# Hybrid decoder block on one core: reordering the state-space octets among the projections

## Chip, core and metric

The kernel runs on one core of one Trainium2 chip. The metric is the device time of one execution in microseconds. Three executions of the kernel before took 2342.69, 2344.36 and 2347.79 us; their median, 2344.36 us, is the time before. Engines are named as in the profile: PE does matrix products (PEld its weight loads), DVE and ACT work on vectors, POOL is GpSimd, SP only issues transfers. SP, ACT and POOL can each issue DMAs, from queues of their own.

## What is computed

One decoder block on a sequence of 512 tokens with 2048 channels: an adaptive norm and one input projection, a diagonal state-space group (S5) and a sparse-attention group side by side, an output projection, and a gated feed-forward part. The change touches the S5 group, the order in which the projections and two "compressions" are put beside it, and some stores of keys and values. The reference of these, cut:

```python
def s5_mixer(u, ...):                      # 64 groups of 16 channels, 64 complex states each
    dt = exp(log_dt); mag = exp(lr * dt)
    ab = mag * cos(li * dt), mag * sin(li * dt)
    den = lr * lr + li * li
    f_re = ((ab_re - 1) * lr + ab_im * li) / den      # the factors of B
    f_im = (ab_im * lr - (ab_re - 1) * li) / den
    bb = f * b                                        # per group 64 x 16
    bu = einsum('bsgh,gph->sbgp', u, bb)
    states = associative_scan(a_l * a_r, a_r * b_l + b_r)   # over the 512 tokens
    y = real(states @ c) + d_skip * u
    z = gelu(y); return z * sigmoid(z @ w_glu + b_glu)

def compress_tokens(kv, pe, w1, w2):       # once for K, once for V
    flat = overlapping blocks of 32 tokens of kv + pe
    return gelu(flat @ w1) @ w2
```

## The kernel before

Weights and activations are f32; every large product is made as three products of halves (hi·hi, lo·hi, hi·lo: L100, L101, L102), so each weight tile `wr` is cast to `wh` on ACT and subtracted to `wl` on DVE (both L75), in two halves of 128x1024 for a projection. The kernel goes through phase A (to about 223 us), phase B1 (to about 499 us), the attention, the output projection, and the feed-forward part. The change lies at the end of phase A and in B1.

**Phase A.** While PE makes the products for `u`, K and V, POOL works from the start on the S5 tables (`s5_prep`, L59): powers of the discretised A, then a normalisation of two pairs of tables on 128x512 tiles (`n1`), the copies into `s5CH` and `s5SH`, and at the very end the three multiplications that finish the factors of B, `s5fr` and `s5fi`, by the reciprocal of `den`. At the end of phase A, four tiles of K (`qk_d`, 512 KB each, from `spill`, L675) and four of V (`v_d`, 256 KB each, L319) are stored to DRAM; these eight stores stand on POOL, behind the tables. They are read from the tiles `adw`, whose memory B1's S5 tiles take over.

**Phase B1.** Twelve projections `proj(i)` of 48 matmuls 128x512 each. Among them eight S5 octets (`s5_octet`, eight groups each). An octet, in the order of the code: `s5bb` and `s5bg`, `s5TT` from the factors of B and the tables (L526 to L549); the octet's C and S tables (`s5C`, `s5S`, `s5x`; L563 to L569); eight transposes (L585) that give `s5W`; `Kt` (16 transposes, L593), which is stored to `k_s` (L599) and read back in a skewed form as the weight `s5w` (L603; named `w3` in the code, one buffer); the bias `bu` from the weight tile `s5wt` and the row `shb` (L610 to L618); the input product E (L625); the scan with a product by a rotated identity (L638); the state `s5SS`; and the output Y (L647 with `s5w`, L648 with `s5SS`), gelu and the store `z_d` (L652). Octets are put after projections 2, 3, 5, 6, 8, 9, 11 by the rule `12 * n < 8 * (i - 1)`, and the last after the loop. `compress(0)` stands ahead of projection 11; then, behind the last octet, `gate` (31 matmuls, L744, L745), `compress(1)` (its transposes are L784, its weights `wh<-in_w_dram`), `gate_tail`.

**What sets the order.** Each engine takes its instructions strictly in one order. A scheduler makes it at build time from dependences and priorities (`high_priority`), with order-only links where the code asks for them (`after`, and `Held`, which links each operation of an engine to one before it). So an instruction that waits holds everything behind it on its engine, also what belongs to other work.

Of the kernel before, what the change touches and what calls it, by code (L numbers as in the profile page):

```python
# [64 lines left out]
class Block:  # L65
    def __init__(self, ctx, tc, a):
        self.ctx, self.tc, self.a = ctx, tc, a
        self.nc = tc.nc
        self.V, self.A, self.T = tc.nc.vector, tc.nc.scalar, tc.nc.tensor


# [8 lines left out]
    def weights(self, src, out=None, first=None):  # L80

        res = []
        with self.tc.high_priority():
            raw = self.wp.tile([P, 2048], F32, name="wr", bufs=2)
            self.nc.sync.dma_start(raw, src)
            for h in range(2):
# [6 lines left out]
                if first is not None:  # L93
                    self.after(parts, first)
                res.append((hi, lo))
        return res
# [114 lines left out]
    def phase_a(self, hh, hl, tab, ps):  # L211
# [4 lines left out]
        with ExitStack() as st:  # L216
# [59 lines left out]
            for kt in range(KT):  # L276
# [4 lines left out]
                if kt >= 8:  # L281
                    hl[kt] = tab.tile([P, S], F32R, name=f"hl{kt}")
                self.modulate(xt[kt], m[:, 1, kt:kt + 1], m[:, 0, kt:kt + 1], rb, hh[kt], hl[kt], pa)
                if kt < 8:
# [22 lines left out]
            for i in range(4):  # L307
                p = pk[i]
                if i == 0:
                    q, t = (pa.tile([P, 8, 64], F32, name="modt", bufs=2).rearrange("p a b -> p (a b)")  # L310
                            for _ in range(2))
                    p = self.rope(p, q, t, self.rot[:, 0], self.rot[:, 1], 64)
                if i % 2 == 0:
                    o = tmp(4).bitcast(F32R)
                self.spill(self.qk_d[0, P * i:P * i + P], p, o[:, 2 * (i % 2):2 * (i % 2) + 2])
            o = tmp(4)
            for t in range(4):
                A.copy(o[:, t], pk[4 + t])
                self.v_spill = nc.gpsimd.dma_start(self.v_d[t], o[:, t])  # L319

# [18 lines left out]
    def s5_prep(self, pool, W):  # L339
# [93 lines left out]
        with tc.high_priority(-100000):  # L433
# [6 lines left out]
            V.tensor_add(den, den, q)  # L440
            self.V.reciprocal(rd, den)
            V.tensor_scalar(nr, ar, -1.0, None, op0=ALU.add)
# [4 lines left out]
            V.tensor_add(fr, fr, q)  # L447
            V.tensor_mul(fr, fr, rd)
            V.tensor_mul(fi, ai, lr)
            V.tensor_mul(q, nr, li)  # L450
            V.tensor_sub(fi, fi, q)
            V.tensor_mul(fi, fi, rd)
            V.tensor_scalar(fi, fi, sgn, None, op0=ALU.mult)
            r8 = pool.tile([P, 64], F32, name="s5r8")
# [28 lines left out]
            powers(CA, SA, fc, fs)  # L483
            n1 = t((P, 8, 64))
            for C, Sn in ((CB, SB), (CA, SA)):

# [21 lines left out]
    def s5_octet(self, o, Tb, W, ps):  # L508
# [5 lines left out]
        U, bc = self.s5_next  # L514
        SS = W.tile([P, 8, 66], F32, name="s5SS")
        V.memset(SS[:, :, 0:1], 0.0)
        bx, cx = bc[:, 0], bc[:, 1]
# [41 lines left out]


        Ch, Sh = C[:, :, 0:4], Sn[:, :, 0:4]
        tc1 = W.tile([P, 8, 8, 8], F32, name="s5x", bufs=4)[:, :, 0:4]
# [5 lines left out]
        V.tensor_mul(tc2, ab(Tb["CH"]), ba(Tb["SB"]))  # L568
        V.tensor_add(Sh, Sh, tc2)  # L569
        for x, sg in ((C, 1.0), (Sn, -1.0)):  # L570
            A.activation(x[0:64, :, 4:8], x[64:P, :, 0:4], AF.Copy, scale=sg)
# [9 lines left out]
        with hp():  # L581
            for q in range(2):
                p = ps.tile([P, 4, P], F32, name="tp", bufs=2)
                for g in range(4):
                    T.transpose(p[:, g], w1[:, 4 * q + g].rearrange("p r i -> p (r i)"), self.ident)  # L585
                A.copy(W1[:, 4 * q:4 * q + 4], p)
        Kt = W.tile([P, 8, 9 * 16], F32, name="s5bg", bufs=3).rearrange("p a b -> p (a b)")
        Kt = Kt[:16, 0:1024].rearrange("p (g x) -> p g x", g=8)
# [53 lines left out]
        V.tensor_mul(z5, z3, Sf)  # L642
        V.tensor_add(SS[:, :, 1:65], z4.rearrange("p (g j) -> p g j", g=8), z5.rearrange("p (g j) -> p g j", g=8))
        with hp():
            Y = ps.tile([P, S], F32, name="acc", bufs=4)
            for g in range(8):
                T.matmul(Y[:, 64 * g:64 * g + 64], w3[:, g], U[:, g], start=True, stop=False)  # L647
                T.matmul(Y[:, 64 * g:64 * g + 64], TT[:, g, 0:8].rearrange("p k h -> p (k h)"), SS[:, g, 0:64],  # L648
                         start=False, stop=True)
            zz = W.tile([P, 8, 64], F32, name="s5x", bufs=4)  # L650
# [21 lines left out]

    def spill(self, dst, q, t, scale=None):
        self.split(q, t[:, 0], t[:, 1], scale)
        self.nc.gpsimd.dma_start(dst, t.bitcast(F32))  # L675

    def phase_b1(self, hh, hl):
        nc, tc, a, V, A, T = self.nc, self.tc, self.a, self.V, self.A, self.T
        with ExitStack() as st:
# [8 lines left out]
            shb = self.shb = W.tile([P, D], F32, name="shb")  # L688
            self.after([nc.gpsimd.dma_start(shb, self.sh_d.to_broadcast([P, D]))], self.v_spill)
            n = 0  # L690

            def octet(n):
                if n:
                    self.s5_next = self.s5_loads(n, SW)
                self.s5_octet(n, self.Tb, SW, ps)

            for i in range(12):
                if i == 11:
                    self.compress(0, W, ps)
                p = self.proj(i, hh, hl, ps)  # L700
                with tc.high_priority():
# [13 lines left out]
                    else:  # L715
# [5 lines left out]
                        self.spill(self.qk_d[g, P * t:P * t + P], p, t2, -0.125)  # L721
                while 12 * n < 8 * (i - 1):
                    octet(n)
                    n += 1
            octet(n)
            gs = self.gate(hh, hl, W, ps)
            self.compress(1, W, ps)
            self.gate_tail(gs, ps)
# [810 lines left out]
```

## Time and profile before

| | |
|---|---|
| median of three runs | 2344.36 us |
| the profiled execution, its own time | 2354.09 us |
| its span in the trace | 2352.3 us |
| PE busy | 2195.6 us, 93% |
| DVE busy | 1854.9 us, 79% |
| ACT busy | 1080.2 us, 46% |
| POOL busy | 309.6 us, 13% |

The profiled execution is one run; its time is 9.73 us above the median of the three others and 1.8 us above its own span. PE's share is that of the whole span: within phase B1 there are stretches with PE at nearly 100% and others with PE near 0, and the rows further below are taken stretch by stretch. "PEclk" in the rows is the granted TensorE clock as a share of full speed: 1.00 is 2.4 GHz, 0.50 is 1.2 GHz.

### The profile page before, as it was taken

How to read it: one execution, taken by the hardware profiler on the slowest of the kernel's cores; microseconds unless marked ns; L12 is line 12 of the kernel's file. 1: busy time of each engine (PE TensorE's matmuls, PEld its weight loads, DVE VectorE, ACT ScalarE, POOL GpSimd, SP SyncE). 2: the span in 40 equal slices, each digit the busy share in tenths (PEclk: the TensorE clock that was granted, in tenths of full speed). 3: DMA queues.
4: the chain of work that ended last, by engine and by line, in shares of the span. 5: the costliest groups of instructions: out<-in, count | busy, mean ns of one | idle time of the engine just before them, and what ended most of it. 6: DMA issues, size and time to landing. Idle time of an engine off the chain costs nothing.

```text
span 2352.3 us, 34734 instructions
## 1 busy us (share of the span) xinstructions
PE 2195.6 (93%) x13694; PEld 1918.0 (82%) x13694; DVE 1854.9 (79%) x2776; ACT 1080.2 (46%) x1823; POOL 309.6 (13%) x376
## 2 busy tenths in 40 slices
PE   7997899878899878899999999999999999999997
PEld 5776778666677666899999999999999788888886
DVE  7896888658988877889999999999999773553436
ACT  3422444348867742744445444454444431221215
POOL 8999111100000011000000000000000000000000
PEclk9999999979999989999999999999999999999998
DMA  9784656576477467233333333333333783443223
GB/s 345 289 284 177 207 167 177 158 209 207 150 239 228 171 258 287 85 123 127 126 129 126 122 122 122 122 121 122 122 121 112 286 310 120 148 145 119 90 90 108
DMA packets 94003, 398.20 MB, mean 169 GB/s; under 512 B 19968, under 2 KB 28448, under 8 KB 58384
## 3 DMA queue, kind: packets, MB, share of 16 engines
q1 hardware_dynamic: 79440, 344.51, 42.0%
q0 software_dynamic: 14400, 51.49, 6.6%
q8 instruction: 107, 1.75, 0.3%
q14 instruction: 56, 0.46, 0.1%
HBM read 358.20 MB, written 37.69 MB: 168 GB/s over the span
## 4 chain that ended last, share of the span: by engine, by line
PE 54%; issue 4%; DVE 3%; ACT 1%; DMA 1%; POOL 1%; POOLq 0%; DVEq 0%; ACTq 0%
PE dn L102 7%; PE dn L100 7%; PE dn L101 6%; PE sa L101 6%; PE sa L100 6%; PE sa L102 6%; PE sb L100 5%; PE sb L102 5%; PE sb L101 5%; DMA adw<-in_wada_dram 0%; DVE wl L75 0%; DMA a_d<-cv 0%; POOL adw L119 0%; POOL x_d L1045 0%; DVE cv L1090 0%
## 5 line engine op out<-in xcount | busy, mean ns | idle before, releaser
L75 ACT CAST wh<-wr 128x1024 fp32r<-128x1024 f32 (+1 forms) x257 | 262.0, 1024 | 502.5 <-PE dn L101 320.5
L75 DVE TENSOR_TENSOR wl<-wr,wh 128x1024 fp32r<-128x1024 f32 (+1 forms) x255 | 307.6, 1210 | 50.1 <-ACT wh L75 38.8
L124 DVE SCALAR_TENSOR_TENSOR adw<-adw,silc 128x2048 f32<-128x2048 f32 x63 | 146.7, 2331 | 26.4 <-DMA adw<-in_wada_dram 25.3
L100 PE MATMUL mm<-yh,wh 128*128 128x512 f32 (+1 forms) x320 | 129.4, 409 | 26.7 <-DVE x L1043 7.8
L75 ACT CAST xh<-wq 128x1024 fp32r<-128x1024 f32 x84 | 88.3, 1052 | 139.2 <-DVE wq L1229 104.2
L75 ACT CAST wh<-wq 128x1024 fp32r<-128x1024 f32 x84 | 88.3, 1052 | 137.8 <-DVE wq L1229 104.5
L1099 POOL DMA_DIRECT2D a_d<-cv x44 | 23.8, 541 | 856.5 <-DVE cv L1098 856.5
L101 PE MATMUL mm<-yl,wh 128*128 128x512 f32 (+1 forms) x320 | 128.8, 403 | 7.4 <-DVE yl L75 7.4
L102 PE MATMUL mm<-yh,wl 128*128 128x512 f32 (+1 forms) x320 | 127.9, 401 | 1.9 <-DVE wl L75 1.9
L1293 DVE SCALAR_TENSOR_TENSOR x<-dn,mod,x 128x512 f32<-128x512 f32 (+1 forms) x56 | 37.6, 673 | 108.3 <-PE dn L102 107.8
L75 DVE TENSOR_TENSOR xl<-wq,xh 128x1024 fp32r<-128x1024 f32 x84 | 102.4, 1218 | 24.2 <-ACT xh L75 24.2
L75 DVE TENSOR_TENSOR wl<-wq,wh 128x1024 fp32r<-128x1024 f32 x84 | 102.2, 1218 | 22.7 <-ACT wh L75 22.7
L100 PE MATMUL dn<-b21h,wh 128*128 128x512 f32 x256 | 101.8, 398 | 3.1 <-ACT wh L75 3.1
L102 PE MATMUL dn<-b21h,wl 128*128 128x512 f32 x256 | 102.1, 399 | 0.5 <-DVE wl L75 0.5
L1229 DVE TENSOR_TENSOR wq<-wq,wr 128x1024 f32<-128x1024 f32 x84 | 102.0, 1215 | 0.1
L101 PE MATMUL dn<-b21l,wh 128*128 128x512 f32 x256 | 101.8, 398 | 0.0
L100 PE MATMUL dn<-t4h,wh 128*128 128x512 f32 (+1 forms) x256 | 97.8, 382 | 0.0
L102 PE MATMUL dn<-t4h,wl 128*128 128x512 f32 (+1 forms) x256 | 97.7, 382 | 0.0
L101 PE MATMUL dn<-t4l,wh 128*128 128x512 f32 (+1 forms) x256 | 97.6, 381 | 0.0
L100 PEld LDWEIGHTS mm<-yh,wh 128*128 128x128 f32 x320 | 62.7, 198 | 41.7 <-issue 16.9
L146 POOL TENSOR_TENSOR rms_r<-rms_v,mhalf 128x2 f32<-128x2 f32 (+1 forms) x8 | 10.8, 1346 | 637.5 <-DVE rms_v L144 637.4
L102 PE MATMUL mm<-hh,wl 128*128 128x512 f32 x192 | 79.5, 414 | 15.9 <-DVE wl L75 15.9
(535 smaller groups left out, 7852.8 us busy)
## 6 DMA issues: line engine op xcount, KB each, us to landing
adw<-in_wada_dram SPq DMA_DIRECT2D x49, 1024.0 KB, 6.7
wr<-in_wup_dram SPq DMA_DIRECT2D x46, 1024.0 KB, 4.9
wq<-in_wup_dram SPq DMA_DIRECT2D x42, 1024.0 KB, 6.8
wr<-in_wdn_dram SPq DMA_DIRECT2D x40, 1024.0 KB, 4.9
wr<-in_wada_dram SPq DMA_DIRECT2D x32, 1024.0 KB, 4.9
wr<-in_wout_dram SPq DMA_DIRECT2D x16, 1024.0 KB, 5.5
adw<-in_wada_dram POOLq DMA_DIRECT2D x14, 1024.0 KB, 7.7
wr<-in_wp_dram SPq DMA_DIRECT2D x12, 1024.0 KB, 5.2
```

What stands on the lines that cost most here:

```text
L75: return self.A.copy(hi, src), self.V.tensor_sub(lo, src, hi.bitcast(F32))
L100: self.T.matmul(ps, wh, xh, start=start, stop=False)
L101: self.T.matmul(ps, wh, xl, start=False, stop=False)
L102: self.T.matmul(ps, wl, xh, start=False, stop=stop)
L124: self.V.scalar_tensor_tensor(t, t, 1.0, self.silc, op0=ALU.mult, op1=ALU.mult, accum_out=out)
L146: self.rms_pow = self.nc.gpsimd.tensor_tensor(r[:, 0:n], v[:, 0:n], self.mhalf.to_broadcast([P, n]), op=ALU.pow)
L1099: self.nc.gpsimd.dma_start(self.a_d[:, m], val)
L1229: V.tensor_add(src, src, add)
L1293: V.scalar_tensor_tensor(x, p, gate, x, op0=ALU.mult, op1=ALU.add)
```

## The change

- `s5_prep` gets a third step. The reciprocal of `den` is put on DVE behind the modulation of K-tile 8 of phase A, and the three multiplications of `s5fr` and `s5fi` stand on POOL ahead of the last normalisation instead of behind the copies.
- The four `qk_d` and four `v_d` stores at the end of phase A are issued by ACT; the load of `shb` is issued by SP, behind the loads of weights and of `rt`.
- In the first octet the C and S tables are linked behind a `wl` of the weights (`self.lo[-2]`), so that the octet begins with `s5bb`.
- `s5_octet` becomes a generator with two stops. Its first part goes to the copies of `s5W`; the second from the state's memset over `Kt`, `s5w`, E and the scan to `s5SS`; the third is Y, gelu and `z_d`. The third part of an octet is written out between the first and the second part of the next. Y's matmuls lose their high priority. The state's memset moves into the second part.
- The octets follow the rule `12 * n < 9 * (i - 1)`: after projections 2, 3, 4, 6, 7, 8, 10, 11. `compress(0)` stands ahead of projection 9, `compress(1)` ahead of projection 11. Behind the loop come `gate`, the Y of the last octet, and `gate_tail`.

The number of matmuls is the same.

```diff
@@ s5_prep @@
-            self.V.reciprocal(rd, den)
...
-            V.tensor_mul(fr, fr, rd)
...
-            V.tensor_mul(fi, fi, rd)
-            V.tensor_scalar(fi, fi, sgn, None, op0=ALU.mult)
...
             n1 = t((P, 8, 64))
+        yield
+        with tc.high_priority(-100000):
+            with tc.high_priority(200000):
+                self.after([self.V.reciprocal(rd, den)], self.modulated)
+            V.tensor_mul(fr, fr, rd)
+            V.tensor_mul(fi, fi, rd)
+            last = V.tensor_scalar(fi, fi, sgn, None, op0=ALU.mult)
+            V = Held(V, lambda i: self.after([i], last))
             for C, Sn in ((CB, SB), (CA, SA)):
@@ phase_a @@
-                self.spill(self.qk_d[0, P * i:P * i + P], p, o[:, 2 * (i % 2):2 * (i % 2) + 2])
+                self.spill(self.qk_d[0, P * i:P * i + P], p, o[:, 2 * (i % 2):2 * (i % 2) + 2], queue=nc.scalar)
...
-                self.v_spill = nc.gpsimd.dma_start(self.v_d[t], o[:, t])
+                nc.scalar.dma_start(self.v_d[t], o[:, t])
@@ s5_octet @@
-        SS = W.tile([P, 8, 66], F32, name="s5SS")
-        V.memset(SS[:, :, 0:1], 0.0)
...
+        if o == 0:
+
+            lo = self.lo[-2]
+            V = Held(V, lambda i: self.after([i], lo))
         Ch, Sh = C[:, :, 0:4], Sn[:, :, 0:4]
...
                 A.copy(W1[:, 4 * q:4 * q + 4], p)
+        yield
+        SS = W.tile([P, 8, 66], F32, name="s5SS")
+        V.memset(SS[:, :, 0:1], 0.0)
...
+        yield
+        Y = ps.tile([P, S], F32, name="acc", bufs=4)
+        for g in range(8):
+            T.matmul(Y[:, 64 * g:64 * g + 64], w3[:, g], U[:, g], start=True, stop=False)
...
         with hp():
-            Y = ps.tile([P, S], F32, name="acc", bufs=4)
...
@@ phase_b1 @@
-            self.after([nc.gpsimd.dma_start(shb, self.sh_d.to_broadcast([P, D]))], self.v_spill)
+            nc.sync.dma_start(shb, self.sh_d.to_broadcast([P, D]))
             n = 0
+            prev = []
...
-                self.s5_octet(n, self.Tb, SW, ps)
+                cur = self.s5_octet(n, self.Tb, SW, ps)
+                next(cur)
+                if prev:
+                    next(prev.pop(), None)
+                next(cur)
+                prev.append(cur)
 
             for i in range(12):
-                if i == 11:
-                    self.compress(0, W, ps)
+                if i in (9, 11):
+                    self.compress((i - 9) // 2, W, ps)
...
-                while 12 * n < 8 * (i - 1):
+                while 12 * n < 9 * (i - 1):
                     octet(n)
                     n += 1
-            octet(n)
             gs = self.gate(hh, hl, W, ps)
-            self.compress(1, W, ps)
+            next(prev.pop(), None)
             self.gate_tail(gs, ps)
```

How this moves instructions on the engines, at three places. First DVE at the end of phase A, before the change: the first octet's memset and tables stand ahead of the projection's second `wl`.

```order
L75 TENSOR_TENSOR adw<-b,adw 128x512 x2
L516 MEMSET s5SS 128x8
L563 TENSOR_TENSOR s5C<-s5CH,s5CB 128x8x32
L564 TENSOR_TENSOR s5x<-s5SH,s5SB 128x8x32
L567 TENSOR_TENSOR s5S<-s5SH,s5CB 128x8x32
L565 TENSOR_TENSOR s5C<-s5C,s5x 128x8x32
L568 TENSOR_TENSOR s5x<-s5CH,s5SB 128x8x32
L75 TENSOR_TENSOR wl<-wr,wh 128x1024
```

The same place after the change (line numbers are those of the changed kernel; its L76 is L75 before, L600 the memset):

```order
L76 TENSOR_TENSOR adw<-b,adw 128x512 x2
L600 MEMSET s5SS 128x8
L532 TENSOR_TENSOR s5bb<-s5bc,s5fr 128x128
L533 TENSOR_TENSOR s5tb<-s5bc,s5fi 128x128
L532 TENSOR_TENSOR s5bb<-s5bc,s5fr 128x128
L533 TENSOR_TENSOR s5tb<-s5bc,s5fi 128x128
L534 TENSOR_TENSOR s5bb<-s5bb,s5tb 128x128
L536 TENSOR_TENSOR s5bb<-s5bb,s5tb 128x128
L538 TENSOR_SCALAR s5bc<-s5bc,cons 128x128
L537 TENSOR_SCALAR s5bb<-s5bb,cons 128x128
L548 TENSOR_TENSOR s5bg<-s5bb,s5PR 128x8x128
L549 TENSOR_TENSOR s5bg<-s5bb,s5PI 128x8x128
```

The next instruction behind these is the `wl` that stood behind the tables before. The memset, which waited for nothing before, now takes memory that the `v_d` stores read, and waits for these. On PE the first octet's eight transposes, which had 77 of the projections' matmuls ahead of them, have 42.

POOL at the end of the tables, before: the factors of B, the eight stores and `shb` stand behind the last copies.

```order
L59 COPY s5SH<-sp_1060 64x256 x2
L59 TENSOR_TENSOR s5fr<-s5fr,sp_1005 128x64
L59 TENSOR_TENSOR s5fi<-s5fi,sp_1005 128x64
L59 TENSOR_SCALAR s5fi<-s5fi,cons 128x64
L675 DMA qk_d<-adw 128x1024 x2
L319 DMA v_d<-adw 128x512
L675 DMA qk_d<-adw 128x1024 x2
L319 DMA v_d<-adw 128x512 x3
L689 DMA shb<-sh_d 128x2048
```

ACT at the end of phase A, after the change: the stores stand between the copies out of PSUM, ahead of the next weights' cast.

```order
L76 CAST adw<-b 128x512 x2
L322 COPY adw<-b 128x512
L690 DMA qk_d<-adw 128x1024 x3
L323 DMA v_d<-adw 128x512
L322 COPY adw<-b 128x512 x2
L323 DMA v_d<-adw 128x512 x2
L322 COPY adw<-b 128x512
L323 DMA v_d<-adw 128x512
L76 CAST wh<-wr 128x1024
```

The stores leave POOL's queue; ACT, on which a waiting issue holds the casts of the weights, takes them over.

PE near the end of B1, before: the Y of the octet before the last (L647) stands directly behind that octet's scan product (L638), in the middle of projection 11's matmuls.

```order
L100 MATMUL mm<-hh_118,wh 128x512
L585 MATMUL tp<-cons,s5bg 128x128 x4
L638 MATMUL acc<-s5x,cons 128x512
L647 MATMUL acc<-s5U,s5w_3630 128x64
L585 MATMUL tp<-cons,s5bg 128x128 x4
L101 MATMUL mm<-hl_1754,wh 128x512
L102 MATMUL mm<-hh_118,wl 128x512
```

PE at the end of B1, after the change: the last matmuls of the gate, the last octet's L652 (L638 before), and its Y.

```order
L764 MATMUL mm<-hl_1754,wh 64x512
L765 MATMUL mm<-hh_118,wh 128x512
L764 MATMUL mm<-hl_1794,wh 64x512
L765 MATMUL mm<-hh_120,wh 128x512
L652 MATMUL acc<-s5x,cons 128x512
L661 MATMUL acc<-s5U,s5w_3813 128x64
L662 MATMUL acc<-s5SS,s5TT 128x64
```

POOL in the same stretch, after the change: the last `s5w` is issued behind the store of the octet before it.

```order
L613 DMA k_s<-s5bg 128x1x128
L690 DMA qk_d<-sp 128x1024
L667 DMA z_d<-s5x 8x128x64
L617 DMA s5w_3813<-k_s 128x8x128
L667 DMA z_d<-s5x 8x128x64
```

The last `s5w` is read into the one buffer that the Y before it still reads, so it comes behind that Y. Before the change, `compress(1)` stood between the gate and the gate's tail; now the last Y stands there, and the Y of the octet before it stands ahead of the gate.

## Rows read from the trace of the kernel before

**Rows 1.** Waits of PE from 205 to 500 us: line, releaser, total us, times, longest.

```profile
PE mm L102 <- DVE wl L75: 15.9, 1, 15.9
PE acc L647 <- DMA s5w<-k_s: 7.9, 1, 7.9
PE tp L784 <- DMA wh<-in_w_dram: 6.3, 1, 6.3
PE acc L638 <- DVE bu L613: 2.7, 1, 2.7
```

**Rows 2.** Stretches: busy us (instructions) by engine, PEclk, DMA share, GB/s.

```profile
223.00:239.00 16.00, 0.07 (x2) 0.03 (x1) 3.79 (x7) 2.18 (x5) 12.56 (x21) 0.64 0.42 156
262.00:446.00 184.00, 176.97 (x965) 143.96 (x963) 156.00 (x265) 84.71 (x181) 23.93 (x27) 0.98 0.60 173
446.00:455.00 9.00, 1.11 (x5) 0.52 (x4) 3.80 (x4) 0.00 (x0) 1.33 (x1) 0.69 0.30 60
455.00:475.00 20.00, 19.66 (x106) 14.26 (x105) 8.56 (x19) 9.72 (x25) 3.73 (x4) 0.88 0.46 127
...
482.00:499.00 17.00, 14.74 (x85) 12.99 (x85) 6.50 (x22) 6.14 (x13) 1.27 (x1) 0.80 0.79 172
330.00:360.00 30.00, 27.62 (x142) 22.73 (x141) 22.24 (x38) 12.98 (x27) 4.32 (x5) 0.89 0.68 196
390.00:420.00 30.00, 29.70 (x160) 24.42 (x158) 27.56 (x46) 11.19 (x24) 4.34 (x5) 1.00 0.70 210
```

**Rows 3.** Timeline of DVE: start, us, line, operation, idle before and releaser.

```profile
216.77 0.07 DVE L516 MEMSET s5SS<- 128x8 f32 x1
...
235.82 0.61 DVE L564 TENSOR_TENSOR s5x<-s5SH,s5SB 128x256 f32<-128x256 f32 x1 [5.63 <-DMA qk_d<-adw]
...
237.71 1.21 DVE L75 TENSOR_TENSOR wl<-wr,wh 128x1024 fp32r<-128x1024 f32 x1
238.84 0.28 DVE L526 TENSOR_TENSOR s5bb<-s5bc,s5fr 128x128 f32<-128x128 f32 x1
...
240.45 1.21 DVE L542 TENSOR_TENSOR s5bg<-s5bb,s5PR 128x1024 f32<-128x1024 f32 x1
```

**Rows 4.** Timeline of PE as it resumes in phase B1.

```profile
242.13 0.63 PE L100 MATMUL mm<-hh,wh 128*128 128x512 f32 x1
242.55 0.63 PE L101 MATMUL mm<-hl,wh 128*128 128x512 f32 x1
...
247.20 0.39 PE L102 MATMUL mm<-hh,wl 128*128 128x512 f32 x1
247.43 0.39 PE L100 MATMUL mm<-hh,wh 128*128 128x512 f32 x1
...
249.48 0.47 PE L102 MATMUL mm<-hh,wl 128*128 128x512 f32 x1
```

**Rows 5.** Timeline of POOL at the tables' end.

```profile
230.75 0.44 POOL L59 TENSOR_SCALAR s5fi<-s5fi,cons 128x64 f32<-128x64 f32 x1
231.13 1.21 POOL L675 DMA_DIRECT2D qk_d<-adw  x2
```

**Rows 6.** DMA from 205 to 262 us: rate in forty slices; issues, KB, us to landing.

```profile
GB/s 414 411 118 0 0 0 0 0 190 425 342 147 0 0 0 0 0 0 0 325 359 362 365 391 285 299 408 288 341 377 410 224 184 0 109 81 158 379 227 350
...
qk_d<-adw POOLq DMA_DIRECT2D x4, 512.0 KB, 4.5
...
v_d<-adw POOLq DMA_DIRECT2D x4, 256.0 KB, 6.4
```

**Rows 7.** Timeline of POOL around the last octet.

```profile
465.70 1.30 POOL L652 DMA_DIRECT2D z_d<-s5x  x1 [1.00 <-ACT s5x L651]
```

**Rows 8.** The weight s5w: its products; us from its issue to landing.

```profile
L647 PE MATMUL acc<-s5U,s5w x128: 219/275/476, 281.3 to 493.5; 128*128 128x64 f32 x128
...
DMA to landing us min/median/max: 7.8/8.9/11.0
```

**Rows 9.** DMA issues from 465 to 500 us.

```profile
Q<-qk_d SPq DMA_DIRECT2D x2, 512.0 KB, 16.1
```

More of the change, by code (lines that the diff above doesn't have):

```diff
@@ L69, in __init__ @@
         self.V, self.A, self.T = tc.nc.vector, tc.nc.scalar, tc.nc.tensor
+        self.lo = []
     def split(self, src, hi, lo, scale=None):
@@ L94, in weights @@
                     self.after(parts, first)
+                self.lo.append(parts[1])
                 res.append((hi, lo))
@@ L282, in phase_a @@
                     hl[kt] = tab.tile([P, S], F32R, name=f"hl{kt}")
-                self.modulate(xt[kt], m[:, 1, kt:kt + 1], m[:, 0, kt:kt + 1], rb, hh[kt], hl[kt], pa)
+                self.modulated = self.modulate(xt[kt], m[:, 1, kt:kt + 1], m[:, 0, kt:kt + 1], rb, hh[kt], hl[kt], pa)
+                if kt == 8:
+                    next(prep)
                 if kt < 8:
@@ L569, in s5_octet @@
         V.tensor_add(Sh, Sh, tc2)
+        V = self.V
         for x, sg in ((C, 1.0), (Sn, -1.0)):
@@ L643, in s5_octet @@
         V.tensor_add(SS[:, :, 1:65], z4.rearrange("p (g j) -> p g j", g=8), z5.rearrange("p (g j) -> p g j", g=8))
-        with hp():
-            Y = ps.tile([P, S], F32, name="acc", bufs=4)
[L646 to L649, printed above, removed]
+        yield
+        Y = ps.tile([P, S], F32, name="acc", bufs=4)
+        for g in range(8):
+            T.matmul(Y[:, 64 * g:64 * g + 64], w3[:, g], U[:, g], start=True, stop=False)
+            T.matmul(Y[:, 64 * g:64 * g + 64], TT[:, g, 0:8].rearrange("p k h -> p (k h)"), SS[:, g, 0:64],
+                     start=False, stop=True)
+        with hp():
             zz = W.tile([P, 8, 64], F32, name="s5x", bufs=4)
@@ L671, in rope, with spill @@
         return q
-    def spill(self, dst, q, t, scale=None):
+    def spill(self, dst, q, t, scale=None, queue=None):
         self.split(q, t[:, 0], t[:, 1], scale)
-        self.nc.gpsimd.dma_start(dst, t.bitcast(F32))
+        (queue or self.nc.gpsimd).dma_start(dst, t.bitcast(F32))
     def phase_b1(self, hh, hl):
```

## The prediction

> **What bounds the kernel now.** I read three views in turn. First the waits of PE over the stretch in which the change lies [rows 1]: one wait of 15.9 us for a `wl`, one of 7.9 for an `s5w`, one of 6.3 for the weights of a compression, one of 2.7 for `bu`. Then the same stretch cut into windows [rows 2], because PE's 93% over the whole span hides them: between 262 and 446 us PE is busy 176.97 of 184, but between 223 and 239 it does 0.07 us of work and between 446 and 455 it does 1.11. So B1 is bound by PE in its middle and by single waits at its opening and its end. Last, the timelines, for who holds what. At the opening DVE reaches a tables operation of the first octet, which takes the memory of a phase-A tile, and waits 5.63 us until that tile's `qk_d` store has landed [rows 3]; the store had only been issued at 231.13, when POOL was through with tables and factors [rows 5]. The `wl` for which PE waits stands behind that operation and runs at 237.71.
>
> A wait costs more than its length. After the first one PE's matmuls start 0.42 us apart (242.13, 242.55) instead of 0.23 (247.20, 247.43) [rows 4]: the granted clock is at 1.2 GHz before it is back at 2.4. Windows show it as PEclk: 0.88 of the 20 us behind the `s5w` wait and 0.80 of the 17 us behind the compression's wait [rows 2]. I charge that as 20 x 0.12 = 2.4 and 17 x 0.20 = 3.4 us.
>
> **The change, part by part.** The profiled execution took 2354.09 us, 9.73 above the median of 2344.36. The sum is made in its time; I assume the same difference in us for the median.
>
> *The Y of each octet goes behind the first part of the next.* The 7.9 us wait is a Y standing directly behind its own scan product while its `s5w` was still landing; from issue to landing that load takes 7.8 to 11.0 us [rows 8]. With the first part of another octet and projection matmuls between them the load is covered for seven of the eight octets: in the trace only one `s5w` wait is listed at all. Removed: 7.9 + 2.4 = 10.3. If the cover were gone, it would be paid again.
>
> *compress(1) goes among the projections.* Its weights were asked for when buffers came free, and PE had only the gate to cover them: 6.3 + 3.4 = 9.7 us. compress(0), which already stood among projections, has no such wait in the list [rows 1], and that is the nearest row for the new place. Removed: 9.7; if the new place has the same wait, 6.3 of it comes back.
>
> *The last Y has nothing behind which to hide.* Its `s5w` has one buffer and comes behind the Y before it; POOL's order puts that Y's `z_d` store ahead of it. From the end of a Y: some 1.1 us to the gelu, 1.30 us of POOL for the store [rows 7], then 7.8 to 11.0 us [rows 8], so 10.2 to 13.4. Beside it PE has the gate, some 32 matmuls at 0.23 = 7.4, and the scan product, about 0.8: 8.2 us. A new wait of 2.0 to 5.2; I take 3.5, and 2 us of slow clock behind it, as the smaller of the two charges above. The attention's first loads fall in the same time, and one of these took 16.1 us [rows 9]: with that, 18.5 - 8.2 = 10.3, and 3.4 of clock, 13.7. Taken: -5.5, bounds -2.0 and -13.7.
>
> *The opening.* The factors are ready well before POOL's tables end, and tables no longer stand ahead of the `wl`. But the memset, which ran at 216.77 without a wait [rows 3], now stands on tiles that the `v_d` stores read, and DVE holds everything behind it until these have landed; the first octet's inputs (`s5bc`, 256 KB) come down SP's queue behind 1,024 KB of weights, 512 KB for `rt` and 1,024 KB for `shb`. Together with the stores (4 x 512 and 4 x 256 KB [rows 6]) that is 5,888 KB, 6.0 MB. While stores and loads ran together in the trace, from 232 on, the rate was 285 to 391 GB/s, mostly about 365 [rows 6]: 16.5 us. They can begin at 211 to 215, as the last products of phase A come off PE, the bulk from 213: landed at 229.5. Then DVE has eight small operations (238.84 to 240.45, 1.6 us), two of 1.1, a `wl` of 1.1 and one more of 1.1 [rows 3]: PE's eight transposes at 235.9. In the new order they have 42 projection matmuls ahead of them, not 77, so 35 more follow, 35 x 0.227 = 7.9 us and 2.6 of slow clock (13 matmuls at 0.2 us more, as now): both are done at 235.9 + 0.9 + 10.5 = 247.3. In the trace the first matmul behind the same work starts at 249.48 [rows 4]. Gain: 2.2 us. PE does not get back the 16 us, only a little of it, since one stalled queue replaces another. Bounds: with all stores at 300 GB/s, 20 us, landed at 233, a loss of 1.3; with the stores' own 3.1 MB served ahead of SP's loads, 8.6 us from 215, landed at 223.5, a gain of 8.2.
>
> The Trainium skill, in "DMA: Bandwidth & Descriptors", section "Issuing engines are not separate DMA queues", says that transfers from any engine's queue run on the same 16 DMA engines and interleave, and that issuing from several engines saves only the time of issuing. By that rule the stores on ACT's queue land mixed with SP's loads, which is the 2.2 us; against it would stand the 8.2. The rate in rows 6 agrees with the rule: with two queues at work from 232 on it is no higher than the 414 GB/s at 205.
>
> *Denser octets.* From 262 to 446 PE has 7.0 us of idle time and PEclk 0.98 (3.7 us). Some of it goes: the 2.7 us wait for `bu`. But octets now follow at 3 in 4 projections instead of 2 in 3, 12% more DVE work for the same PE stretch. In the densest window, 390 to 420, DVE is busy 27.56 beside 29.70 of PE, a ratio of 0.93 [rows 2]. Twelve per cent more with no more PE work would make 1.04, with the octet's own PE work counted about 0.98: no slack, and with in-order queues on both sides small waits in each octet. At 1.04 about 165 us of PE would grow by 7 or 8; without a wait and at full clock 5 would be won. I take -2.5.
>
> *The rest.* The reciprocal and three POOL operations cost under 2 us and only change places on POOL, which no later wait names. Phases behind B1 are the same instructions, and B1 still ends with a Y: the last product with `s5w` starts at 493.5 in the trace [rows 8]. Zero.
>
> Sum: 10.3 + 9.7 - 5.5 + 2.2 - 2.5 = 14.2 us less: 2339.9 for the profiled execution, 2330 against the median. The deviations of single terms (-3.5/+6.0 opening, -8.2/+3.5 last Y, -5.5/+7.5 density, -6.3 compression) combine as squares to -12/+10: 2320 to 2342.
>
> **The rivals.**
> *The stores land early.* ACT's stores get ahead of SP's loads; the memset stops at 223.5 and the opening wins 8.2: 2324. For it: the DMA queues move nothing from 209 to 216 us [rows 6]. Against it: the rate's ceiling, and SP's weights asked for at the same time.
> *The last Y collides.* Its `s5w` lands as late as the attention's loads: 8.2 us of the gain go, 2338.5.
> *The waits only move.* The order puts Y and compress(1) elsewhere, but their loads are issued later as well, since the single `s5w` buffer and the weights' buffers come free later too. The 20 us come back as waits in the middle, of the kind of the 2.7 us one: about 2344.
> *DVE becomes the bound (slower).* Place: the octets from 262 us on. Y now stands, without priority, between the first and second part of the next octet, so PE and DVE alternate in one chain: first part, Y, second part. DVE has 156.0 + 3.8 + 8.6 = 168 us of work from 262 to the last octet's state [rows 2]. In the forecast that state is there at about 471, a busy share of 168/209 = 0.80; now it is 156/184 = 0.85 in the middle, but 22.24/30 = 0.74 in the window from 330 to 360. The point from which it decides is 168/223 = 0.755: below it the state comes later than 485, and nothing is won. At 0.72 the state comes at 495: 10 us slower than now, 2354.
>
> **How the numbers follow.** Forecast, 2330 (2320 to 2342): 0.60. Stores early, 2324: 0.10. Last Y collides, 2338.5: 0.12. Waits only move, 2344: 0.08. DVE bound, 2354: 0.10. A measurement of this kernel can tell about 0.2%, 4.7 us, from no change. Faster by more, under 2339.7: 0.57 of the forecast's 0.60, the early stores, two thirds of the collision: 0.75. Slower: 0.10. The same: 0.15. The range goes from 2318, the lower half of the early stores, to 2345, which takes in the waits that only move; outside it lie the DVE bound and the forecast's and the early case's own ends, together about 0.2.
>
> **What would show it.** In the changed trace: the memset of `s5SS` on DVE starting at 229 to 231 behind a `v_d` store, and PE's idle time before the first `s5bg` transposes 13 to 16 us; no wait of PE for the compression's weights; one `s5w` wait, of the last Y, of 2 to 5 us; DVE's share in the octets 0.80 to 0.85; the gate's transposes some 14 us earlier than now. The prediction is wrong if the opening's wait ends before 225 or after 235, if PE waits for DVE in the octets sum up to over 15 us, or if `s5w` is waited for in more than the last octet.

## The result and the profile after

The changed kernel is slower: 2368.26 us (2359.29 to 2374.24, five runs) against 2347.79 us (2342.69 to 2349.42, five runs), a ratio of 1.0078 with a 95% interval from 1.0053 to 1.0104. Run again beside three of the experiments, on one chip with them, it was 1.0062 (1.0039 to 1.0085). The forecast was 2330 us against a median of 2344.36 of three of the runs before, and its range ended at 2345. The profiled execution after took 2374.24 us, 20.2 more than the one before.

First, where B1 ends: the transposes behind the gate, of the kernel before and of the changed one (line, operation, number, ns of one, first to last start).

```profile
L758 PE MATMUL tp<-cons,qr x4: 223/223/261, 494.5 to 494.7; 48*128 48x48 f32 x4
...
L778 PE MATMUL tp<-cons,qr x4: 303/303/339, 512.5 to 512.9; 48*128 48x48 f32 x4
```

B1 ends 18.0 us later, not 14.2 earlier: of the 20.1 us between the two spans (2372.4 and 2352.3 us) 18.0 are lost by the end of B1. The waits of PE from 205 to 520 us, the changed kernel's answer to [rows 1]:

```profile
PE tp L596 <- DVE s5bg L550: 25.2, 3, 16.2
PE acc L652 <- DVE s5x L649: 9.5, 4, 6.8
PE tp L607 <- DVE s5TT L555: 8.7, 2, 8.6
PE acc L639 <- ACT s5U L635: 5.6, 1, 5.6
PE acc L661 <- DMA s5w<-k_s: 3.5, 1, 3.5
```

The compression's weights are gone from the list, and of the `s5w` waits only that of the last Y is left, 3.5 us. The 16.2 us, the longest wait of the first line, are the opening. But in the octets PE now waits 9.0, 9.5, 8.7 and 5.6 us, most of it for DVE. The same stretch in one window, before, changed, and the changed kernel with one buffer moved (experiment e1, below); columns as in [rows 2]:

```profile
262.00:475.00 213.00, 197.74 (x1072) 158.75 (x1070) 168.37 (x287) 94.43 (x206) 28.99 (x32) 0.96 0.57 164
...
262.00:475.00 213.00, 182.20 (x967) 150.01 (x966) 154.77 (x261) 82.18 (x172) 24.06 (x27) 0.92 0.57 155
...
262.00:475.00 213.00, 203.35 (x1126) 167.45 (x1124) 170.30 (x290) 94.27 (x200) 27.81 (x31) 0.98 0.59 165
```

In the changed kernel both engines do less in the same time: PE 182 instead of 198, DVE 155 instead of 168. DVE is not overloaded, it stands still. What for, its own list says (changed kernel, DVE from 205 to 520 us, the largest total):

```profile
DVE s5x L647 <- DMA z_d<-s5x: 23.4, 5, 9.0
```

The longest of the five, in the timelines of POOL, DVE and PE of the changed kernel (start, us, line, operation, idle before and releaser):

```profile
350.74 1.34 POOL L617 DMA_DIRECT2D s5w<-k_s  x1 [9.26 <-PE acc L661]
352.19 1.29 POOL L667 DMA_DIRECT2D z_d<-s5x  x1
...
366.06 0.69 DVE L647 TENSOR_TENSOR s5x<-s5x,s5S 128x512 f32<-128x512 f32 x1 [9.01 <-DMA z_d<-s5x]
366.67 1.35 DVE L555 TENSOR_TENSOR s5TT<-s5TT,s5bg 128x1152 f32<-128x1152 f32 x1
...
368.17 3.57 PE L607 MATMUL tp<-s5TT,s5bb 128*16 128x128 f32 x16 [8.56 <-DVE s5TT L555]
```

L647 is the second product ahead of the scan. It wants one of the four `s5x` buffers, and the free one is that of the output of the octet before (`zz`), which its `z_d` store still reads. The store was issued at 352.19, behind the load of the next `s5w`, which takes its place on POOL as soon as the Y has read the old one; it is done at 366. Behind L647 in DVE's queue stand `s5TT` of the next octet, for which PE's transposes wait, and the weights' `wl`. In the order before, a store had the next octet's whole first part to land in; now the output comes between the first and the second part, and only Y's own successors lie between.

### The profile page after: what moved, and what is told of

It reads as the page before. It is cut to its first block, busy times and chain, and to the rows that moved or that the text cites. A ratio compares the mean times of both kernels' runs of the same rounds, so it can differ in the third digit from the quotient of the medians.

```text
span 2372.4 us, 34736 instructions
## 1 busy us (share of the span) xinstructions
PE 2203.7 (93%) x13694; PEld 1925.9 (81%) x13694; DVE 1855.3 (78%) x2776; ACT 1081.1 (46%) x1823; POOL 304.2 (13%) x367
## 4 chain that ended last, share of the span: by engine, by line
PE 65%; DVE 7%; issue 6%; DMA 4%; ACT 3%; POOL 1%; POOLq 0%; DVEq 0%; ACTq 0%
PE dn L104 6%; PE dn L102 6%; PE dn L103 6%; PE sa L103 6%; PE sa L102 6%; PE sa L104 6%; PE sb L102 5%; PE sb L104 5%; PE sb L103 5%; PE mm L102 2%; PE mm L104 2%; PE mm L103 2%; DMA z_d<-s5x 2%; PE s L907 1%; PE tp L939 1%
## 5 line engine op out<-in xcount | busy, mean ns | idle before, releaser
L76 ACT CAST wh<-wr 128x1024 fp32r<-128x1024 f32 (+1 forms) x257 | 262.0, 1024 | 506.9 <-PE dn L103 320.6
L76 DVE TENSOR_TENSOR wl<-wr,wh 128x1024 fp32r<-128x1024 f32 (+1 forms) x255 | 308.2, 1213 | 49.5 <-ACT wh L76 43.6
L76 ACT CAST xh<-wq 128x1024 fp32r<-128x1024 f32 x84 | 88.4, 1052 | 139.2 <-DVE wq L1249 104.0
L76 ACT CAST wh<-wq 128x1024 fp32r<-128x1024 f32 x84 | 88.2, 1052 | 138.0 <-DVE wq L1249 104.9
L76 DVE TENSOR_TENSOR xl<-wq,xh 128x1024 fp32r<-128x1024 f32 x84 | 102.5, 1220 | 24.3 <-ACT xh L76 24.3
L76 DVE TENSOR_TENSOR wl<-wq,wh 128x1024 fp32r<-128x1024 f32 x84 | 102.4, 1220 | 22.9 <-ACT wh L76 22.9
L1307 DVE TENSOR_TENSOR x<-x,dn 128x512 f32<-128x512 f32 x32 | 21.9, 685 | 91.5 <-PE dn L104 91.5
```

The source lines that it names most:

```text
L76: return self.A.copy(hi, src), self.V.tensor_sub(lo, src, hi.bitcast(F32))
L1307: V.tensor_add(x, x, p)
```

## The experiments

All ratios are to the kernel before on the same chip. "B1 ends" is the start of the last product with `s5w` or of the transposes behind the gate, whichever is later, in the one profiled execution; "z_d" is the sum of DVE's waits for that store in B1 (times).

| kernel | z_d, us | B1 ends, us | ratio (95% interval) |
|---|---|---|---|
| before | 0 | 494.5 | 1 |
| changed | 23.4 (5) | 512.5 | 1.0078 (1.0053 to 1.0104) |
| changed again | 20.0 (5) | 508.5 | 1.0062 (1.0039 to 1.0085) |
| e6, store issued by ACT | 16.8 (4) | 502.8 | 1.0017 (1.0001 to 1.0033) |
| e20, store ahead of s5w on POOL | 10.0 (3) | 495.3 | 1.0000 (0.9981 to 1.0020) |
| e14, output in s5C | 20.6 (2) | 498.5 | 1.0028 (1.0014 to 1.0043) |
| e1, output in qt | 0 | 475.0 | 0.9948 (0.9927 to 0.9969) |
| e21, output in qt, store ahead of s5w | 0 | 482.6 | 0.9977 (0.9955 to 0.9998) |
| e4, outputs not deferred | 0.8 (1) | 489.1 | 0.9959 (0.9939 to 0.9979) |
| e2, octets at their old places | 24.4 (7) | 523.2 | 1.0139 (1.0105 to 1.0173) |
| e3, compressions at their old places | 19.4 (5) | 512.6 | 1.0084 (1.0052 to 1.0116) |

Three theories at first: A, the buffer held by the store; B, too much DVE work since the octets are denser; C, the compressions among the projections.

**e1: the output in another buffer.** The buffer `qt` is used by two projections after the first, and by the compressions.

```
-            zz = W.tile([P, 8, 64], F32, name="s5x", bufs=4)
+            zz = self.zw.tile([P, S], F32, name="qt").rearrange("p (g j) -> p g j", j=64)
```

> The changed kernel, but the gelu's output is put into the buffer of another tile (qt, which only three projections use) and no longer into one of the four s5x buffers. Theory A (the scan's products take the s5x buffer that the z_d store of the octet before still reads, DVE waits for that store with all behind it): the five waits of DVE for z_d at L647, 23.4 us, go, and with them PE's waits of 2.2, 8.6, 6.8, 2.4 us and part of the 6.8 one, some 20 us and 3 to 5 of slow clock: 2340 to 2348. Theory B (DVE has too much work per projection since the octets are denser): at most 5 us, above 2360. Theory C (compressions among the projections): no change, 2362 to 2370.

The z_d waits are gone, PE's waits in the octets fall to some 10 us, B1 ends at 475.0:

```profile
L779 PE MATMUL tp<-cons,qr x4: 303/303/339, 475.0 to 475.4; 48*128 48x48 f32 x4
```

A holds. By the ratio the gain is larger than expected (0.9948, where 2340 to 2348 us would be 0.997 to 1.000), and the kernel before is beaten by 0.5%. The longest that is left, 4.2 us at L652 at 301.26, is not the store's: DVE had waited 6.6 us for a load of `s5bc` before it.

**e2 and e3: density and compressions undone, the buffer as changed.**

```
-                while 12 * n < 9 * (i - 1):
+                while 12 * n < 8 * (i - 1):
...
+            octet(n)
             gs = self.gate(hh, hl, W, ps)
```

> The changed kernel with the octets at their old places (after projections 2, 3, 5, 6, 8, 9, 11 and the last behind the loop), all else as changed. Theory A: a z_d store still stands between one octet's output and the next octet's scan, with sometimes a projection more in between; some waits for z_d stay, 5 to 12 us are won: 2354 to 2362. Theory B: the waits go, 2335 to 2348. Theory C: 2362 to 2370.

Far slower, with the z_d waits at 24.4 us in seven places. The octets' density is not the cause; B falls. That it would be still slower no theory had expected.

```
-                if i in (9, 11):
-                    self.compress((i - 9) // 2, W, ps)
+                if i == 11:
+                    self.compress(0, W, ps)
...
             next(prev.pop(), None)
+            self.compress(1, W, ps)
             self.gate_tail(gs, ps)
```

> The changed kernel with the first compression ahead of projection 11 and the second behind the gate and the last output, as before. Theory A: the z_d waits stay; PE's 5.7 us for the projection weight that landed late beside the compression's loads go, the 6 us for the compression's weights come back: 2362 to 2372. Theory B: likewise. Theory C: 2345 to 2355.

No different from the changed kernel; C falls.

**e4: each output behind its own state again.**

```
-                next(cur)
-                if prev:
-                    next(prev.pop(), None)
-                next(cur)
-                prev.append(cur)
+                for _ in cur:
+                    pass
```

> The changed kernel with each octet's output directly behind its own state again and at high priority. Theory A: the z_d store is issued a whole octet's first part earlier than the next scan, so the z_d waits at L647 go (under 5 us together), but one or more waits for s5w of 4 to 8 us come back, also in the middle: 2345 to 2356. Theory B: DVE's work is as dense, 2360 to 2370. Theory C: 2362 to 2370.

The z_d waits go with the deferral and two s5w waits of 10.5 us together come back, as A has it. So the deferral trades one store for one load. Here too the kernel before is beaten.

**e5: the opening alone, in the kernel before**, and the changed kernel once more beside it. e5's edit is the first part of the change's diff (`s5_prep`, `phase_a`, `Held` in the first octet, `shb`); the octets keep their code:

```
+                if kt == 8:
+                    next(prep)
...
+                nc.scalar.dma_start(self.v_d[t], o[:, t])
...
+            nc.sync.dma_start(shb, self.sh_d.to_broadcast([P, D]))
```

> The kernel before with the first part of the change alone: factors of B ahead of the last tables, the stores of K and V on ACT, shb on SP, the first octet beginning with the factors. The octets, their outputs and the compressions stay as before. Theory A (all of the loss comes from the z_d store and the s5x buffers in the octets): 2 to 3 us at the opening as predicted, and no z_d wait: 0.997 to 1.001 of before. Rival (the opening disturbs the octets behind it): above 1.003.

1.0040 (1.0016 to 1.0063), on the rival's side: no z_d wait of note (3.4 us), but three s5w waits of 25.5 us together in the profiled execution, which was the slowest of its twelve (2354.34 to 2378.67). The likely reason is that the opening shifts the octets against their loads, and in the old order a Y stands right behind its s5w; the shift was not tested by itself.

> The changed kernel once more, beside the next three on one chip. All theories: 1.005 to 1.010 of the time of before.

**e6 and e20: the same buffer, the store sooner.** e6 issues it from ACT behind the gelu, e20 leaves it on POOL and puts the next `s5w` behind it:

```
-            nc.gpsimd.dma_start(self.z_d[o]...
+            nc.scalar.dma_start(self.z_d[o]...      # e6
...
+        if o:
+            self.after([w3_load], self.z_store)     # e20
```

> The changed kernel with the z_d stores issued by ACT right behind the gelu, not by POOL behind the load of s5w; the output keeps its s5x buffer. Theory A with the store's queue as the cause of its length (landing up to 13.8 us behind the s5w load on POOL's queue): the waits of DVE at L647 fall from 23.4 us to under 8, and the time to 0.994 to 1.000 of before, near the kernel with the buffer moved. Rival (the buffer is held for the store however it is issued): the waits stay above 15 us, 1.003 to 1.008.

> The changed kernel with one order link more: POOL issues the load of an octet's s5w behind the z_d store of the octet before it, and no longer ahead of it; the output stays in its s5x buffer. Theory A, with the store's landing time as the price (6.5 us in the middle, up to 13.8, behind 512 KB of s5w): the store lands in 3 to 5 us, DVE's waits at L647 fall from 20 to 23 us to under 8, 10 to 15 us are won, 0.998 to 1.003 of before. Rival (the store is late since the DMA engines are shared and the buffer is wanted too early in any case): the waits stay above 14 us, 1.004 to 1.009.

DVE's waits for the store in e6 and e20 (total us, times, longest), and the time of the eight stores from issue to landing in the kernel before, the changed one and e20:

```profile
DVE s5x L647 <- DMA z_d<-s5x: 16.8, 4, 9.6
...
DVE s5x L649 <- DMA z_d<-s5x: 10.0, 3, 4.6
...
DMA to landing us min/median/max: 5.7/6.7/9.6
...
DMA to landing us min/median/max: 5.9/10.2/13.8
...
DMA to landing us min/median/max: 5.5/7.6/9.8
```

Neither run is wholly on one side: in e6 the waits stay above the rival's 15 us while the ratio lies between the two forecasts; in e20 the ratio is theory A's, and the waits lie between. The 6.5 us in the middle that e20's expectation names take in loads from `z_d` too; the stores alone have 10.2.

e20 is the cleanest of the experiments. The scheduler can put instructions in another order in each variant, and a changed order is a rival to the store as the cause. In the traces of the changed kernel and of e20, though, DVE, ACT and PE carry out the same instructions in the same order from 216 us to the end of B1 (347, 233 and 1271 of them); only POOL issues the store and the `s5w` load the other way round. With that alone the stores land sooner, DVE's waits for them are halved and the loss is gone. In e1 36 of DVE's 347 instructions stand elsewhere in the order, in e6 90 and in e14 78, so what e1 gains beyond e20 may be the buffer, the order or both; no run separates them.

The queue is thus part of the price (10.2 us in the middle and up to 13.8 as changed, 7.6 and 9.8 in e20); that the buffer is wanted too early is the rest, by theory A. Across changed, e6, e20 and e1 the waits fall from 20 or 23 to 17, 10 and 0 us, and the ratio from 1.007 to 1.002, 1.000 and 0.995.

**e14: the output in a table of its own octet**, since `qt` is not clean: in e1 the compressions waited 2.3 us for it, in other kernels with it up to 11.4.

```
+            zz = C.rearrange("p g a b -> p g (a b)")
```

> The changed kernel, with the gelu's output put into the octet's own table s5C, which is dead by then and has two buffers, in place of a fourth of s5x; no other tile is touched (the qt buffer of the earlier runs is also the compressions', whose loads then waited for it). Theory A: no wait of DVE for z_d in the octets, B1's last transposes at 470 to 478 us (475.0 with qt, 508.5 and 512.5 as changed), 0.990 to 0.996 of before. Rival (the gain with qt came from something else, such as another order of the scheduler): B1 ends after 490, above 1.000.

The expectation that DVE would not wait was wrong, and the end of B1 and the ratio fell on the rival's side. Since the store still holds DVE, the run does not decide between the two:

```profile
DVE s5C L573 <- DMA z_d<-s5C: 20.6, 2, 10.3
```

The tables of the octet after next come so early in DVE's order that they want that buffer at the same time. The same store holds the same engine in two places instead of five, and less than half of the loss remains: 1.0028. The sum of the waits alone, then, does not set the loss. And moving the output is not enough; it has to go to a buffer that nothing early in the queue takes.

**e8: the opening's hole closed.** On top of e1 all of the first octet's vector work is linked behind the weights of projection 1 (and the second octet's first part).

```
+        if o < 2:
+            lo = self.lo[3]
+            V = Held(V, lambda i: self.after([i], lo))
...
         V = self.V
+        if o == 0:
+            first = self.lo[3]
+            V = Held(V, lambda i: self.after([i], first))
```

> The kernel with the output in the other buffer (e1), and all of the first octet's vector work, memset and bias included, linked behind the weights' halves of projection 1 (and the second octet's first part too). Theory (the opening's 16 us on PE is DVE's queue held at the memset with the projections' weights behind it, not a lack of work): PE runs through projections 0 and 1 while the stores land, its wait at the opening falls from 16.3 to under 6 us, 8 to 13 us and 2 us of slow clock below e1: 0.988 to 0.992 of before. Rival (the loads that the projections need arrive late as well): the wait only moves to a matmul of a projection, 0.993 to 0.997.

PE's 16.3 us at the opening are gone (4.3 us for a weight is the longest wait there), and nothing is won, as the rival had it: B1 ends at 478.6 and the ratio is 0.9965 (0.9944 to 0.9986), no better than e1. The first octet's Y starts at 273.6 instead of e1's 281.5, but later waits, 5.7 us for a `wl` in a projection among them, take the lead back. Why was not settled.

**e15, e17, e18: single parts beside e14**, and e10 to e13, the same beside the `qt` buffer. Their edits are those above put together: e15 is e14 with e5's lines taken back, e17 is e14 with e3's, e18 the kernel before with e14's line; e10 is the kernel before with e1's line, e11, e12 and e13 are e1 with the opening, the density and the compressions taken back; e21 is e1 with e20's link.

> As e14, with the opening as before. If the opening is worth its predicted 2.2 us: B1 ends 1 to 5 us after e14. If it costs: earlier than e14. If the 20 us seen with qt were the opening's and not the qt collision's (11.4 us of waits there): over 10 us after e14.

1.0053 (1.0034 to 1.0071), B1 ends at 503.1, 4.6 us after e14: the new opening is worth some 5 us there.

> As e14, with the compressions at their old places. If the move is worth its predicted 9.7 us: B1 ends 6 to 13 us after e14, with a wait of PE for the compression's weights of 4 to 8 us. If not: within 3 us of e14.

1.0013 (0.9996 to 1.0030), B1 ends at 497.7, 0.8 us before e14. The wait for the compression is back, 5.8 us, but the last Y's 5.8 us for s5w is gone, since the compression covers it again. The move is worth nothing there.

> The kernel before, with only the gelu's output moved into s5C. Theory A (in the old order the store has landed by the time its buffer is wanted): nothing to win, 0.997 to 1.003 of before, B1 ending at 488 to 500 us. Rival (the buffer cost the kernel before as well): below 0.995.

1.0012 (0.9987 to 1.0037): in the kernel before there is nothing to win by the buffer, as theory A had it, though 114 of DVE's 345 instructions up to the end of B1 changed places with it. Its profiled execution, with B1 ending at 508.0, was the slowest of a wide spread (2339.73 to 2367.60).

> The kernel before, with only the gelu's output moved from the s5x buffers to the qt buffer. Theory A as it stands (the buffer is held at the wrong time only since the output comes between the next octet's first and second part): nothing to win here, 0.998 to 1.002 of before, B1 ending at 490 to 500 us as now. Rival (the z_d store costs the kernel before as much, unseen): below 0.996.

> The changed kernel with the output in the qt buffer, and the opening as before (factors behind the tables, stores on POOL, first octet begins with the tables). If the opening is worth the 2.2 us of the prediction: B1 ends 1 to 5 us later than with the new opening (475.0 us), 0.994 to 0.998 of before. If it costs (as it seemed alone in the old order): B1 ends earlier and the time is below 0.993.

> The changed kernel with the output in the qt buffer, and the octets at their old places. Theory A (the density of the octets is no cost once DVE is not held by the store): B1 ends later than 475 us, since the last octet comes behind the loop and nothing stands beside its chain: 485 to 500 us, 0.996 to 1.004 of before. Rival B (density costs): B1 ends before 473 us.

> The changed kernel with the output in the qt buffer, and the compressions at their old places. If moving compress(1) among the projections is worth the 9.7 us of the prediction: B1 ends at 482 to 490 us instead of 475.0, 0.997 to 1.001 of before. If its weights are in time at the old place as well (the wait went away for another reason): within 3 us of 475.

e10: 1.0047 (1.0025 to 1.0069); e11: 1.0012 (0.9996 to 1.0028); e12: 1.0017 (0.9998 to 1.0036); e13: 1.0053 (1.0036 to 1.0070). B1 ends at 515.0, 495.0, 490.1 and 501.1. In all four PE waits for the compressions' loads into `qt` (8.6 us in e10, 11.4 in e11, 5.8 in e12, and 9.2 and 4.6 in e13), so they say little on the part that they undo. e10's wait stands directly ahead of the gate's transposes, in a profiled execution that was the second slowest of its twelve:

```profile
514.05 1.03 PE L803 MATMUL tp<-qt 128*31 128x64 f32 x8 [8.61 <-DMA qt<-in_w_dram]
```

Of the expectations only e12's held (theory A). e10 missed its 0.998 to 1.002, e11's B1 ends 20 us after e1's and not 1 to 5, and e13's is later than either case had it. They suggest that `qt` is a good place only with the whole changed order around it.

> The changed kernel with the output in the qt buffer and the same order link. Theory A: DVE no longer waits for the store in either case, so the link wins nothing more in the octets, and delays s5w by some 2 us, which only the last output can feel: 0.993 to 0.998 of before. If the store's place in POOL's queue costs something beyond the buffer: below 0.992.

0.9977 (0.9955 to 0.9998), as theory A had it: the link adds nothing once the buffer is free. DVE no longer waits for the store; the compressions wait 11.9 us for `qt` here.

## Why the prediction was wrong

**Right, by its own steps.** The opening: the memset behind the `v_d` stores was put at 229 to 231, PE's transposes at 235.9.

```profile
229.86 0.07 DVE L600 MEMSET s5SS<- 128x8 f32 x1 [13.18 <-DMA v_d<-adw]
...
236.71 1.94 PE L596 MATMUL tp<-cons,s5bg 128*128 128x128 f32 x8 [16.23 <-DVE s5bg L550]
```

The memset comes at 229.86 where the sum had 229.5, not at the 223.5 of stores that go ahead of SP's loads, and the hole is as long as before. The rule that the prediction cites from the Trainium skill, in "DMA: Bandwidth & Descriptors", section "Issuing engines are not separate DMA queues", agrees with the 229.86. Behind the same 77 projection matmuls and eight transposes PE goes on at 247.56, against 249.48 before [rows 4]: 1.9 us won where the sum had 2.2. (Its four operations of 1.1 us end at 235.5 as written; the rows' 1.21 us give its 235.9.) At the end of B1, e15 beside e14 makes the opening worth about 5 us. The s5w waits of the other octets did go.

**Right in part by luck: the last Y.** A new wait of 2.0 to 5.2 us was forecast, 3.5 taken; it is 3.5, and 4.4 when run again. But from the end of the Y before it to the landing of `s5w` it took 15.9 us, not 10.2 to 13.4: the load itself took 13.9, outside the 7.8 to 11.0. PE's work and a wait for DVE beside it took 12.4 us and not 8.2, and the two errors cancel.

**Mis-sized: compress(1), 9.7 us.** Its own wait went as said. But another came: at 433.8 PE waits 5.65 us for `s5U` on ACT, which stood behind a weight's cast. The weight's load was issued at 419.72, behind the last products of compress(0), and landed late, while compress(1)'s loads ran beside it from 425 us on.

```profile
432.29 1.04 ACT L76 CAST wh<-wr 128x1024 fp32r<-128x1024 f32 x1 [9.74 <-DMA wr<-in_wp_dram]
433.24 0.16 ACT L633 COPY ub<-acc 128x8 f32<-128x8 f32 x1
```

The wait is there again when the kernel is run again (5.3 us) and in e20 (5.5), but not in e1, e6 and e14, whose compressions stand at the same places, so the place alone does not bring it. And the compression had been the last Y's cover. e17 beside e14 has the move and the last Y together at 0, where the sum had 9.7 - 5.5 = 4.2.

**Failed: "The Y of each octet goes behind the first part of the next", 10.3.** This step counted what the deferral removes, an s5w wait of 7.9 us and its slow clock, and put what it adds at nothing. It never asked what the deferred output carries along: a store, which holds one of four `s5x` buffers until it lands, issued on POOL behind an s5w load that the same Y releases. The prediction did use the order of z_d and s5w on POOL, but for the last octet only. The removal came: that wait is gone, and 10.5 us of such waits come back in e4, where the outputs aren't deferred. In its place DVE waits 23.4 us for the store, in five places, and PE 22 us behind these: 2.2, 8.6, 6.8 and 2.4 us, and about 2.0 of another 6.8 at 304.89, ahead of which DVE had also waited 7.1 us for a load of `s5bc`. The step "Denser octets", -2.5 with -8 as its bound, was where the sum looked for waits in the octets. It counted DVE's work per projection, and the density was not the cause (e2, e4). One of the prediction's own signs of being wrong came up: PE's waits for DVE in the octets sum to 9.0 + 9.5 + 8.7 = 27.2 us, over its 15.

A rough account of B1: against the sum it lost 14.2 + 18.0 = 32.2 us. PE's waits in the octets are 33 us, as against about 8 before for the same lines, 25 more; PEclk over 262 to 475 is 0.92 instead of 0.96, 8.5 us more of slow clock if all of the stretch is charged, as the prediction did. That is 34, and the 22 us behind the store are the largest part.

The rival "DVE becomes the bound" had the sign, the place and the point of decision: DVE's share over 262 to 475 is 154.77/213 = 0.73, below its 0.755. But its mechanism, too much alternating work, isn't what happened: in e20, in exactly the same order, the share is 164.85/213 = 0.77 and the loss is gone, and in e1, as dense, it is 170.30/213 = 0.80, with the best time of all. It got 0.10, and the price named, 10 us, was half of what came.

## What to carry to other kernels

When a piece of work is moved, list the buffers that it holds until its DMAs land, and who in the new order asks for the next buffer of that ring; a store off the critical path becomes the bound when an in-order engine needs its source buffer. Moving a step also uncovers what it had covered: price both ends. Ordering the small store ahead of the large load, with nothing else in another order on PE, DVE and ACT, turned this change from 0.6 to 0.8% slower into even (e20); moving the output to another buffer, with some reordering along with it, made it 0.5% faster (e1).

## What the runs showed of the hardware

Two things were not expected. A `z_d` store of 256 KB took from 5.9 to 13.8 us to land in the changed kernel, where POOL issues most of them right behind a 512 KB s5w load, and 5.5 to 9.8 in e20, where it issues them ahead of that load. And the feed-forward part, which no variant touches, runs at two speeds: 100 us of it, of the kernel before and of e8, with PE busy throughout and the clock granted in full (columns as in [rows 2]):

```profile
1300.00:1400.00 100.00, 99.96 (x872) 98.98 (x871) 93.98 (x105) 49.92 (x58) 2.69 (x5) 1.00 0.33 119
...
1300.00:1400.00 100.00, 99.99 (x857) 99.01 (x856) 91.43 (x101) 48.36 (x56) 2.70 (x5) 1.00 0.35 123
```

872 matmuls against 857; over the whole part this is some 10 us, seen in the profiles of e2, e3, e4, e5, e6 and e8 and in no other. Its cause is open. It is why the places of B1's end are compared above and not the spans of single executions, and the ratios of many runs beside them. Whether the other executions of these six kernels have it isn't known; if all of them do, their ratios above are up to 0.4% too high.
